# Linear attention's second pass and the output weight splits tied to every fourth step of the attention, and an own buffer for context queries

## The chip, the cores and the metric

The kernel runs on one core of a Trainium2 chip. The core has five engines with a queue of instructions each: TensorE (PE: matmuls, with PEld for its weight loads), VectorE (DVE), ScalarE (ACT), GpSimd (POOL) and SyncE (SP, which here issues most of the DMAs). The metric is the device time of one launch in microseconds. A profiled execution gives a span (first to last instruction) and the durations and waits of single instructions.

## The reference, cut to what matters

A two-layer backbone over 2048 latent tokens behind a prefix of 256 context tokens, width 1024, float32. The change lies in the even layer's mixer, where two head groups run side by side and one output projection reads both:

```
a_x = block_attention(q_x, concat([k_x, k_c]), concat([v_x, v_c]), scale)   # 8 heads, latent tokens see all
a_c = block_attention(q_c, k_c, v_c, scale)                                 # context tokens see context alone
b_x, b_c = gla_bidirectional(latent inputs, context inputs)                 # 4 heads, gated linear attention
y = dot(concat([a * silu(za), rms_norm(b) * silu(zb)]), w_out)
```

`gla_bidirectional` runs a gated recurrence over the chunks forwards and another backwards, the context first in both, and adds the two outputs. `rms_norm` is taken per head of 128.

## The kernel before, in words

The 2304 tokens are 18 tiles of 128. All stages are emitted by one Python program into a scheduler that simulates a timeline: of what is ready in that simulation it takes, for each engine, what was emitted first. The order of each engine's queue, SP's and POOL's too, is fixed by that before the run; on the chip an instruction waits on semaphores at its place, and everything behind it in its queue waits with it. `issue_after(x)` adds one rule: what is emitted inside it, on the engine of x, comes behind x in that engine's queue.

**Attention** (`even_attention`, L867). Four head pairs j, and for each five query blocks nb: the context block (256 queries, 2 key tiles) and four latent blocks (512 queries, 18 key tiles). That is 74 steps a head pair and 296 in all. A step handles one key tile for both heads of the pair: three matmuls a head into a bank "st" (L980 to L982; high and low parts of split operands), the exponential on ACT into one of 14 "apt" tiles (L984, recorded under the helper's line L106), and one addition a head on DVE into the running sums "acc" (L971). The value products "av" (`tail`, L922) follow four steps at a time, when six steps are pending (L992). At the end of a block come "den" (L854) and the division (L859 to L863). Queries load into tile "aq" (L910, L911), which has two slots for all blocks: a load can start when the block before the one before it is done. Key and value tiles load on SP too (L885, L892, L899).

**Linear attention** (`gla`, L686). A first pass goes over the 18 tiles (L714 to L795): gates, decays, the products inside a chunk, and for each tile c a state increment D{c}; rotated queries and the inner output are stored to memory (gQ, gO). Two scans turn the increments into states: forwards on POOL with tile "gsf", backwards on DVE with tile "gsb" (both two slots, L804 to L820). The **second pass** (L821 to L846) then goes over the tiles in backward order, context first. For each: three loads (gQ, gO and the gate half of Un), four matmuls of queries with D{c} (L830), the addition (L831), square (ACT) and reduction (L835), a power of two POOL operations (L200, L202), two products (L838 on DVE, L839 on POOL), four transposes (L842), four scaled copies on ACT into a readout tile that has tag "gsb" as well (L845, recorded under L106), and a store to RT (L846). L830 and L842 use the two banks "gl".

**Output weight splits** (L1028 to L1041). Sixteen pieces of 128x512 of the output weights are loaded into one buffer "wraw" (L380), rounded on ACT, and their rest is taken on DVE (L383). The parts go into tiles that linear attention has left: "gu", "gG", "gqt" and others of its first pass, then D{c} in the order in which the second pass reads them, and the last ones into a new pool "woX".

**Order around the change** (`even_mix`, L1009). The attention is a generator. Its loads and first queries are emitted, then all of linear attention (L1025), then all splits, and then the attention's 20 blocks. What was emitted first goes first where it is ready, so the attention fills what linear attention leaves. From block 18 on (n == 18, L1043) the loop also emits the gate's load and the projection of the two context tiles, which lie in slots of "aq".

Of the kernel before, what the change touches and what calls it, by code (L numbers as in the profile page):

```python
# [10 lines left out]
F32 = mybir.dt.float32  # L11
F32R = mybir.dt.float32r
AF = mybir.ActivationFunctionType
ALU = mybir.AluOpType
# [3 lines left out]
P = 128  # L18
D = 1024
KD = D // P  # L20
# [68 lines left out]
class Kern:  # L89
# [596 lines left out]
    def gla(self, gp, gs, g1, gd, pp, tag):  # L686

        nc = self.nc
# [129 lines left out]

        scan(list(range(NT)), slice(0, 64), nc.gpsimd, "gsf")
        scan(self.back_order(), slice(64, 128), nc.vector, "gsb")  # L820
        for c in self.back_order():  # L821
            qT = self.tl(gs, [P, H, P], "gqT")
            nc.sync.dma_start(qT[:].rearrange("p h t -> p (h t)"), self.gQ[c])
            oi = self.tl(gs, [P, 512], "goi")
            nc.sync.dma_start(oi[:], self.gO[c])
            zb = self.tl(gs, [P, H, P], "gsf")[:].rearrange("p h t -> p (h t)")
            nc.sync.dma_start(zb, self.Un[c, :, 1056:])
            ps = bank()
            for h in range(H):
                nc.tensor.matmul(ps[:, h * P : h * P + P], qT[:, h, :], Dl[c][:, h, :], start=True, stop=True)  # L830
# [7 lines left out]
            nc.vector.tensor_tensor(out=o3, in0=o3, in1=ss[:].unsqueeze(2).to_broadcast([P, H, P]), op=ALU.mult)  # L838
            g.tensor_tensor(out=oi[:], in0=oi[:], in1=zb, op=ALU.mult)  # L839
            ps = bank()  # L840
            for h in range(H):
                nc.tensor.transpose(ps[:, h * P : h * P + P], oi[:, h * P : h * P + P], self.ident[:])  # L842
            ro = self.tl(gs, [P, H, P], "gsb")
            for h in range(H):
                self.act(ro[:, h, :], ps[:, h * P : h * P + P], AF.Copy, scale=gn[:, h : h + 1])  # L845
            nc.sync.dma_start(self.RT[4:8, :, c * P : c * P + P].rearrange("j p t -> p j t"), ro[:])  # L846


    def finish(self, av, dacc, zt, dst, w, ap, pp, tag, lnp=None, bufs=(1, 2), out=None):
# [14 lines left out]
        (out or nc.sync).dma_start(dst, rc[:, :w])  # L864
        return rc

    def even_attention(self, ap, pp):  # L867
# [38 lines left out]

        def queries(j, q0, w):

            q = self.tl(ap, [P, 4, 512], "aq", F32R, bufs=2)
            nc.sync.dma_start(q[:A_QK, :, :w].bitcast(F32), self.QT[2 * j : 2 * j + 2, :, :A_QK, q0 : q0 + w].rearrange("h z p t -> p (h z) t"))  # L910
            return q, nc.sync.dma_start(q[A_QK : A_QK + 1, 0::2, :w].bitcast(F32),  # L911
                                        self.QT[2 * j : 2 * j + 2, 0, A_QK : A_QK + 1, q0 : q0 + w].rearrange("h p t -> p h t"))

        pend, late, O = [], [], {}

# [25 lines left out]
        for j in range(4):  # L941
# [12 lines left out]
            for nb, (q0, w, kts) in enumerate(blocks):  # L954
# [10 lines left out]
                def add(n, pts):  # L965
                    for i in range(2):
                        if n == 0:
                            first[i] = pts[i]
                        else:
                            a = first[i] if n == 1 else acc[i]  # L970
                            nc.vector.tensor_tensor(out=acc[i][:, :w], in0=a[:, :w], in1=pts[i][:, :w], op=ALU.add)  # L971

                for n, kt in enumerate(kts):
                    pts = []
# [2 lines left out]
                    for i in range(2):  # L977
                        qh, ql = Q[:, 2 * i, :], Q[:, 2 * i + 1, :]
                        ps = self.tl(pp, [P, 512], "st", bufs=3)
                        nc.tensor.matmul(ps[:, :w], kh[: A_QK + 1, i, kq], qh[: A_QK + 1, :w], start=True, stop=False)  # L980
# [3 lines left out]
                        self.act(pt[:, :w], ps[:, :w], AF.Exp, scale=A_SCALE)  # L984
                        pts.append(pt)
                    add(n, pts)
                    if n == len(kts) - 1:
# [21 lines left out]
    def even_mix(self, e1, win, hT):  # L1009
# [3 lines left out]
        with ExitStack() as es:  # L1013
            with ExitStack() as esa:
# [5 lines left out]
                with ExitStack() as esg:  # L1020
                    gp = self.pool(esg, "glC", side="right", reuse_waits="tile")
                    gs = self.pool(esg, "glS", bufs=2, side="right", reuse_waits="tile")
                    att = self.even_attention(ap, pp)
                    next(att)
                    self.gla(gp, gs, g1, gd, pp, "gl")  # L1025
                ld = self.pool(es, "woX", bufs=2, side="right", reuse_waits="tile")
                w = {}
                places = [(g1, t) for t in ("gG", "gqt", "gkt", "gkT", "gat", "tri")] + [(gd, f"D{c}") for c in self.back_order()]  # L1028
                for u in range(2 * KD):
                    if u < 2:  # L1030
                        x = self.tl(g1, [P, 1056], "gu", F32R)
                        place = x[:, :512], x[:, 512:1024]
                    elif u < 14:
                        place = [self.tl(q, [P, 512], t, F32R, bufs=1)[:] for q, t in places[2 * u - 4 : 2 * u - 2]]
                    else:
                        place = [self.tl(ld, [P, 512], "wo" + z, F32R)[:] for z in "hl"]
                    n, k = divmod(u, KD)
                    for _ in self.split_steps(w, (k, n), None, self.i["w_out0"][:, k : k + 1, n * 512 : n * 512 + 512], 1, 512, None, 1,
                                              stage=(ap, 1, 512), place=[p.unsqueeze(1) for p in place]):
                        pass  # L1040
# [720 lines left out]
```

## Time and profile before

| | us |
|---|---|
| median of 3 runs | 3669.73 |
| lowest and highest run | 3668.54, 3671.02 |
| the profiled execution's own time | 3676.2 |
| its span | 3674.1 |

The attention stage lies at about 1080 to 1990 us of the span. Linear attention's first pass ends at about 1587, the second pass's last store is issued at 1861.5, and the last "av" group of the attention runs from 1968.7 to 1972.3. Of the page, the busy times show which engine is full; the windows of a stretch show the same for part of the span, with the granted clock of TensorE beside it; a row of the timeline shows an instruction's start, its duration, and in brackets the idle time of its engine just before it with what ended that. "L106" is the helper that issues every ACT operation, so ACT rows go by their tiles.

### The profile page before, as it was taken

The page shows a single profiled execution, that of the slowest core. Times are in us where ns is not written, and L with a number is a line of the kernel's source. Part 1 is how long each engine was busy: PE and PEld are TensorE (multiplying, and loading weights), DVE is VectorE, ACT ScalarE, POOL GpSimd, SP SyncE. Part 2 cuts the span into 40 slices and gives each one's busy share as a digit, 9 for nine tenths or more (in the row PEclk, how much of TensorE's full clock was granted, in tenths as well). Part 3 has the DMA queues.
Part 4 walks back from the last instruction along what each step waited for, and adds up shares of the span by engine and source line. Part 5 has one row for each costly group of instructions (what it writes and reads, how often), then busy time and mean ns, then how long its engine had stood idle before and what let it go on. Part 6 is the DMA issues. An engine that isn't in the chain of part 4 may idle for free.

```text
span 3674.1 us, 51831 instructions
## 1 busy us (share of the span) xinstructions
PE 3565.7 (97%) x18404; PEld 2758.7 (75%) x18404; DVE 2363.0 (64%) x4860; ACT 1437.0 (39%) x2741; POOL 1205.6 (33%) x1336
## 2 busy tenths in 40 slices
PE   8999999999999999999999999999899999999998
PEld 6988998888886666655556878888688887555577
DVE  4677666888876666687664444454578784666721
ACT  5545551111125555555553124444422223555510
POOL 1433330101111212122201233333334443777743
PEclk9999999999999999999999999999999999999899
DMA  7455472222241232243622544455744447788554
GB/s 253 145 155 155 133 210 87 80 73 88 75 137 53 83 98 79 85 115 109 177 67 96 188 161 123 141 157 160 227 146 122 146 120 190 210 215 219 175 178 149
DMA packets 364372, 512.19 MB, mean 139 GB/s; under 512 B 25825, under 2 KB 243889, under 8 KB 358210
## 3 DMA queue, kind: packets, MB, share of 16 engines
q1 hardware_dynamic: 322642, 425.49, 39.8%
q0 software_dynamic: 19872, 55.92, 5.1%
q10 hardware_dynamic: 21600, 27.46, 2.1%
q8 instruction: 146, 2.39, 0.3%
q14 instruction: 112, 0.92, 0.1%
HBM read 329.38 MB, written 179.37 MB: 138 GB/s over the span
## 4 chain that ended last, share of the span: by engine, by line
PE 69%; issue 15%; POOL 5%; DVE 5%; DMA 4%; ACT 2%; SPq 0%; POOLq 0%; DVEq 0%; ACTq 0%
PE av L922 7%; PE gm L129 6%; PE gm L130 6%; PE gm L131 6%; PE st L980 4%; PE st L981 4%; PE st L982 4%; PE st L129 2%; PE st L131 2%; PE st L130 2%; PE pj L131 2%; PE pj L130 2%; PE pj L129 2%; PE o L1456 2%; DMA wraw<-w_od 1%
## 5 line engine op out<-in xcount | busy, mean ns | idle before, releaser
L971 DVE TENSOR_TENSOR acc<-acc,apt 128x512 f32<-128x512 f32 x512 | 364.8, 737 | 153.5 <-ACT apt L106 150.6
L106 ACT ACTIVATE apt<-st 128x512 f32<-128x512 f32 (+1 forms) x592 | 344.6, 594 | 290.5 <-PE st L982 257.4
L662 DVE TENSOR_REDUCE mm<-mx 128x1 f32<-128x512 f32 (+1 forms) x656 | 393.2, 630 | 89.9 <-PE mx L661 81.8
L922 PE MATMUL av<-apt,av 128*64 128x512 f32 (+1 forms) x1184 | 286.4, 599 | 0.0
L980 PE MATMUL st<-aq,akh 97*128 97x512 f32 (+1 forms) x592 | 255.7, 432 | 9.7 <-DMA aq<-QT 6.1
L661 PE MATMUL mx<-mk,mq 96*128 96x512 f32 (+1 forms) x656 | 238.6, 372 | 0.0
L981 PE MATMUL st<-aq,akh 96*128 96x512 f32 (+1 forms) x592 | 236.7, 400 | 0.0
L982 PE MATMUL st<-aq,akl 96*128 96x512 f32 (+1 forms) x592 | 235.3, 398 | 0.0
L1330 DVE CUSTOM_DVE_ANT_1 mx<-mx,mtab 128x217 f32<-128x217 f32 (+11 forms) x576 | 184.6, 338 | 49.2 <-PE mx L1324 37.9
L106 ACT ACTIVATE opt<-opt 128x930 f32<-128x930 f32 (+9 forms) x144 | 119.2, 830 | 248.0 <-POOL opt L1627 141.0
L106 ACT ACTIVATE u<-gm 128x352 f32<-128x352 f32 (+1 forms) x144 | 70.5, 496 | 360.4 <-PE gm L131 208.7
L1587 DVE TENSOR_TENSOR opt<-st,tab 128x64 f32<-128x64 f32 (+10 forms) x576 | 142.8, 316 | 88.2 <-PE st L1424 58.1
L922 PEld LDWEIGHTS av<-apt,av 128*64 128x64 f32 x1184 | 81.9, 138 | 156.4 <-issue 154.8
L980 PEld LDWEIGHTS st<-aq,akh 97*128 97x128 f32 x592 | 113.5, 192 | 101.6 <-issue 49.5
L1462 POOL TENSOR_TENSOR oacc<-oacc,opt 128x682 f32<-128x682 f32 (+10 forms) x144 | 169.8, 1199 | 26.4 <-ACT opt L106 25.1
L982 PEld LDWEIGHTS st<-aq,akl 96*128 96x128 f32 x592 | 114.6, 194 | 25.8
L661 PEld LDWEIGHTS mx<-mk,mq 96*128 96x128 f32 x656 | 122.7, 188 | 11.7
L981 PEld LDWEIGHTS st<-aq,akh 96*128 96x128 f32 x592 | 115.3, 195 | 18.3
L1423 PE MATMUL st<-q,kt 128*128 128x480 f32 (+5 forms) x256 | 99.6, 391 | 23.8 <-DVE opt L1587 18.9
L106 ACT ACTIVATE x<-px,modB,modA 128x128 f32<-128x128 f32 x272 | 99.3, 469 | 58.1 <-PE px L331 46.3
L129 PE MATMUL gm<-w0h,hhi 128*128 128x512 f32 x288 | 116.1, 403 | 0.0
L129 PE MATMUL gm<-w1h,hhi 128*128 128x512 f32 x288 | 115.7, 402 | 0.0
(570 smaller groups left out, 9928.1 us busy)
## 6 DMA issues: line engine op xcount, KB each, us to landing
q<-Q SPq DMA_DIRECT2D x48, 512.0 KB
H<-x ACTq DMA_DIRECT2D x36, 512.0 KB
adaw<-ada_w SPq DMA_DIRECT2D x64, 256.0 KB
x<-H SPq DMA_DIRECT2D x32, 512.0 KB
wraw<-w_od SPq DMA_DIRECT2D x64, 256.0 KB
K1t<-okt POOLq DMA_DIRECT2D x32, 512.0 KB, 7.6
kt<-K1t SPq DMA_DIRECT2D x32, 512.0 KB
mtab<-rpb_q SPq DMA_DIRECT2D x16, 899.0 KB
```

The source lines that it names most:

```text
L106: return self.nc.scalar.activation(out, in_, func, **kw)
L129: self.nc.tensor.matmul(out, lh(k), rh(k), start=j == 0, stop=False)
L130: self.nc.tensor.matmul(out, lh(k), rl(k), start=False, stop=False)
L131: yield self.nc.tensor.matmul(out, ll(k), rh(k), start=False, stop=j == n - 1)
L661: mm = nc.tensor.matmul(ps[:, :w], q[:A_QK, (t % 6) * P : (t % 6) * P + P], k[:A_QK, k0 : k0 + w], start=True, stop=True)
L662: nc.vector.tensor_reduce(out=m[:, t, n : n + 1], in_=ps[:, :w], axis=AX.X, op=ALU.max)
L922: nc.tensor.matmul(O[j, nb][i * 64 : i * 64 + 64, :w], V[j, kt // TT][:, kt % TT, i * 64 : i * 64 + 64], pts[i][:, :w], start=n == 0, stop ...
L971: nc.vector.tensor_tensor(out=acc[i][:, :w], in0=a[:, :w], in1=pts[i][:, :w], op=ALU.add)
L980: nc.tensor.matmul(ps[:, :w], kh[: A_QK + 1, i, kq], qh[: A_QK + 1, :w], start=True, stop=False)
L981: nc.tensor.matmul(ps[:, :w], kh[:A_QK, i, kq], ql[:A_QK, :w], start=False, stop=False)
L982: mm = nc.tensor.matmul(ps[:, :w], kl[:A_QK, i, kq], qh[:A_QK, :w], start=False, stop=True)
L1330: nc.vector.tensor_tensor_reduce(out=s, in0=s, in1=tb[:, ri : ri + rn, ci : ci + cn], scale=1.0, scalar=-3e38, op0=ALU.add, op1=ALU.max, a ...
```

## The change

The second pass becomes a generator in two halves a tile: `enter` (matmuls, addition, square, reduction, power) and `leave` (products, transposes, copies, store), with `fetch` for the loads. One turn of it does `leave` of the tile before, `enter` of this tile, and `fetch` of the next. The weight splits become a generator that splits the piece loaded a turn ago and loads the next. A third generator, `later`, strings both together: six turns of weights, then the second pass with a turn of weights beside every second one, then the rest of the weights.

The attention calls a hook behind every step. From step 166 on, at every fourth, the hook takes one turn of `later`. What it emits on PE, ACT and DVE comes behind the step's last score matmul, its second exponential and its last addition; SP and POOL have no such rule. The first pass and the scans are emitted as before. The context block's queries get a tile "aqc" of their own (256 wide, one slot), and "aq" with its two slots is left to the 512-wide blocks. The gate's load comes behind the last query load on SP.

```diff
@@ gla
-        for c in self.back_order():
+        def fetch(c):
             qT = self.tl(gs, [P, H, P], "gqT")
...
             nc.sync.dma_start(zb, self.Un[c, :, 1056:])
+            return c, qT, oi, zb
+        def enter(c, qT, oi, zb):
             ps = bank()
...
             self.rpow(ss[:], ss[:], 1.0 / 128, EPS)
+            return c, oi, zb, ss
+        def leave(c, oi, zb, ss):
             o3 = oi[:].rearrange("p (h t) -> p h t", h=H)
...
+        def second():
+            order = self.back_order()
+            old, cur = None, fetch(order[0])
+            for c in order[1:] + [None, None]:
+                if old:
+                    leave(*old)
+                old = enter(*cur) if cur else None
+                cur = fetch(c) if c is not None else None
+                yield
+        return second()
@@ even_attention
-            q = self.tl(ap, [P, 4, 512], "aq", F32R, bufs=2)
...
+            q = self.tl(ap, [P, 4, w], "aq" if w == 512 else "aqc", F32R, bufs=2 if w == 512 else 1)
...
+                    hook(mm, ex)
@@ even_mix
+                def hook(mm, ex):
+                    count[0] += 1
+                    if count[0] >= 166 and count[0] % 4 == 2:
+                        with self.tc.issue_after(mm.ins), self.tc.issue_after(ex.ins), self.tc.issue_after(self.add.ins):
+                            next(slow, None)
+                def weights():
...
+                    for u in range(2 * KD + 1):
+                        if raw is not None:
...
+                            self.project_split(raw[:], *place)
+                        if u < 2 * KD:
+                            n, k = divmod(u, KD)
+                            raw = self.tl(ap, [P, 512], "wraw", bufs=1)
+                            nc.sync.dma_start(raw[:], self.i["w_out0"][:, k, n * 512 : n * 512 + 512])
+                        yield
+                def later():
+                    ws = weights()
+                    for _ in range(6):
+                        next(ws)
+                        yield
+                    for n, _ in enumerate(second):
+                        if n % 2 and n < 18:
+                            next(ws)
+                        yield
+                    esg.close()
+                    ld.append(self.pool(es, "woX", bufs=2, side="right", reuse_waits="tile"))
+                    for _ in ws:
+                        yield
+                att = self.even_attention(ap, pp, hook)
+                next(att)
+                second, slow = self.gla(gp, gs, g1, gd, pp, "gl"), later()
                 early = []
                 for n, last in enumerate(att):
                     if n == 18:
-                        gate = self.gate_load(0, 1, self.att_free[:].rearrange("p i w -> p (i w)")[:, :D].bitcast(F32))
+                        for _ in slow:
+                            pass
+                        ld = ld[0]
+                        with self.tc.issue_after(self.qload.ins):
+                            gate = self.gate_load(0, 1, self.att_free[:].rearrange("p i w -> p (i w)")[:, :D].bitcast(F32))
```

More of the change, by code (lines that the diff above doesn't have):

```diff
@@ L865, in finish, with even_attention @@
         return rc
-    def even_attention(self, ap, pp):
+    def even_attention(self, ap, pp, hook):
         nc = self.nc
@@ L970, in add @@
                             a = first[i] if n == 1 else acc[i]
-                            nc.vector.tensor_tensor(out=acc[i][:, :w], in0=a[:, :w], in1=pts[i][:, :w], op=ALU.add)
+                            self.add = nc.vector.tensor_tensor(out=acc[i][:, :w], in0=a[:, :w], in1=pts[i][:, :w], op=ALU.add)
                 for n, kt in enumerate(kts):
@@ L1019, in even_mix @@
                 g1 = self.pool(es, "glA", bufs=2, side="right", reuse_waits="tile")
[L1020 to L1040, printed above, removed]
+                esg = ExitStack()
@@ new lines, in even_mix @@
+                gp = self.pool(esg, "glC", side="right", reuse_waits="tile")
+                gs = self.pool(esg, "glS", bufs=2, side="right", reuse_waits="tile")
+                count, ld, w = [0], [], {}
+                def hook(mm, ex):
[3 more added lines that the diff above has]
+                            next(slow, None)
@@ new lines, in weights @@
+                def weights():
+                    places = [(g1, t) for t in ("gG", "gqt", "gkt", "gkT", "gat", "tri")] + [(gd, f"D{c}") for c in self.back_order()]
+                    raw = None
+                    for u in range(2 * KD + 1):
+                        if raw is not None:
+                            if u < 3:
+                                x = self.tl(g1, [P, 1056], "gu", F32R)
+                                place = x[:, :512], x[:, 512:1024]
+                            elif u < 15:
+                                place = [self.tl(q, [P, 512], t, F32R, bufs=1)[:] for q, t in places[2 * u - 6 : 2 * u - 4]]
+                            else:
+                                place = [self.tl(ld[0], [P, 512], "wo" + z, F32R)[:] for z in "hl"]
+                            n, k = divmod(u - 1, KD)
+                            w[k, n] = [p.unsqueeze(1) for p in place]
+                            self.project_split(raw[:], *place)
[4 more added lines that the diff above has]
+                        yield
```

9 lines of the change are left out of this document (5 added, 4 removed).

## The prediction

> **What bounds the kernel now.** I read the page's head first, then the busy time by stretch of the attention stage (about 1080 to 1990 us of the span), then the waits of TensorE, and then the instructions on both sides of each wait.
>
> ```profile
> span 3674.1 us, 51831 instructions
> PE 3565.7 (97%) x18404; PEld 2758.7 (75%) x18404; DVE 2363.0 (64%) x4860; ACT 1437.0 (39%) x2741; POOL 1205.6 (33%) x1336
> ```
>
> TensorE is the bound of the whole, and a change that moves work without removing any can only win where TensorE stands still or runs at a lower clock. The stage by stretches (columns: us, then busy time and instructions of PE, PEld, DVE, ACT, POOL, then granted clock, DMA share, GB/s):
>
> ```profile
> 1080.00:1587.00 507.00, 503.41 (x2581) 321.10 (x2580) 336.15 (x477) 278.06 (x555) 108.52 (x107) 0.99 0.31 88
> 1587.00:1690.00 103.00, 97.73 (x405) 56.94 (x405) 92.66 (x135) 49.87 (x94) 15.91 (x13) 0.92 0.27 75
> 1690.00:1770.00 80.00, 80.00 (x385) 50.00 (x384) 58.27 (x89) 48.55 (x104) 22.65 (x23) 1.00 0.61 170
> 1770.00:1790.00 20.00, 15.16 (x73) 9.07 (x71) 7.62 (x13) 6.93 (x16) 4.81 (x6) 0.83 0.83 207
> 1790.00:1865.00 75.00, 75.00 (x360) 46.70 (x360) 56.65 (x84) 46.57 (x100) 22.27 (x22) 1.00 0.42 119
> 1865.00:1990.00 125.00, 125.00 (x534) 74.99 (x531) 66.18 (x97) 57.73 (x95) 8.22 (x6) 1.00 0.15 48
> ```
>
> The losses sit in two stretches, 1587 to 1690 and 1770 to 1790; in the others PE is full. The four waits behind them, each the instruction that came after the pause, with the idle time and its releaser in brackets:
>
> ```profile
> 1566.95 0.47 PE L980 MATMUL st<-aq,akh 97*128 97x512 f32 x1 [1.24 <-DMA aq<-QT]
> 1598.22 0.50 PE L980 MATMUL st<-aq,akh 97*128 97x512 f32 x1 [1.55 <-ACT apt L106]
> 1674.80 2.07 PE L830 MATMUL gl<-D,gqT 128*128 128x128 f32 x8 [3.71 <-ACT gsb L106]
> 1782.14 0.77 PE L980 MATMUL st<-aq,akh 97*128 97x512 f32 x1 [4.84 <-DMA aq<-QT]
> ```
>
> I call them A, B, C and D. Together 1.24 + 1.55 + 3.71 + 4.84 = **11.3 us** idle. After B, C and D the clock falls as well (same columns as above; the clock is the third number from the end):
>
> ```profile
> 1590.00:1600.00 10.00, 8.45 (x36) 4.36 (x33) 9.69 (x16) 5.03 (x11) 2.23 (x3) 0.95 0.32 100
> 1600.00:1610.00 10.00, 10.00 (x38) 5.14 (x37) 9.78 (x15) 3.48 (x7) 2.65 (x2) 0.70 0.29 79
> 1650.00:1660.00 10.00, 10.00 (x44) 6.02 (x44) 9.65 (x15) 5.31 (x10) 0.00 (x0) 1.00 0.00 0
> 1670.00:1680.00 10.00, 6.29 (x21) 5.07 (x20) 7.83 (x13) 5.75 (x15) 0.00 (x0) 0.71 0.27 79
> 1680.00:1690.00 10.00, 10.00 (x41) 4.95 (x40) 4.34 (x8) 3.37 (x9) 2.92 (x3) 0.78 0.12 28
> 1780.00:1790.00 10.00, 7.86 (x29) 4.90 (x29) 1.98 (x3) 2.39 (x4) 1.02 (x2) 0.66 0.76 192
> ```
>
> Missing clock times length: B (0.05 + 0.30) x 10 = 3.5, C (0.29 + 0.22) x 10 = 5.1, D 0.34 x 10 = 3.4, **12.0 us** in all, which I count as time lost (an upper end). So 23.3 us of the stage are lost at four places. That is the most that the change can win if it adds nothing.
>
> **The change part by part.**
>
> *The context buffer (A and D).* Each head pair starts with a 256-wide context block of two steps, whose queries held one of the two "aq" slots. So the first 512-wide block's queries could load only when the block before the context block was done.
>
> ```profile
> 1771.16 10.89 DMA aq<-QT
> 1724.09 0.45 SPq L910 DMA_DIRECT2D aq<-QT  x1
> ```
>
> The first row is the chain's: the load took 10.89 us, beside two short steps. The second is the load issued one slot earlier, for the context block of the last head pair: it went out some 45 us ahead of its use. With a buffer of its own for context, the slot sequence moves by one: the 512-wide queries go out at that earlier place, and their 10.89 us lie beside a whole block of 18 steps. Block and load stay the same size, so nothing is added but SBUF. The rows show nothing that would be late next. Gain: 1.24 + 4.84 + 3.4 = **9.5 us**. On SP the context loads now queue no later than before.
>
> *The weight splits (B).* One step loads a piece (SP), rounds it on ACT and subtracts on DVE, 16 times. Now load and split of a piece are one call, four steps, apart.
>
> ```profile
> 1597.05 0.63 ACT L106 ACTIVATE gkt<-wraw 128x512 fp32r<-128x512 f32 x1 [2.63 <-DMA wraw<-w_out]
> 1673.60 1.14 ACT L106 ACTIVATE gsb<-gl,gn 128x128 f32<-128x128 f32 x4 [3.98 <-DVE gsb L815]
> ```
>
> The first row is B: ACT waited 2.63 us for a piece with the step's exponentials queued behind, and TensorE then waited for those. Four steps of distance are about 9.5 us (below), which is more than 2.63. So this wait goes: **5.0 us** (1.55 + 3.5). The 16 rounds and 16 subtractions stay and move.
>
> *The second pass (C).* The second row is C: the copies of the first readout tiles use the slots of tile "gsb", which the backward scan on DVE (L814 to L816) also uses. They were put in ACT's order at the place where the scan was expected to be done, and the scan came 3.98 us late. Now the pass begins later. Where, comes from the count of L982, two per step (column x):
>
> ```profile
> 1080.00:1587.00 507.00, 123.79 (x314) 0.99 0.31 88
> 1612.00:1662.00 50.00, 16.59 (x42) 1.00 0.22 63
> 1690.00:1770.00 80.00, 23.65 (x60) 1.00 0.61 170
> ```
>
> At 1587, when the first pass ends, 314 / 2 = 157 steps are done. A step without second-pass work takes 50 / 21 = 2.38 us. The first call is at step 166 (about 1608), six calls go to the weights, so the first matmuls of the pass come at step 190 (1587 + 33 x 2.38 = 1666) and the first copies at step 194 (1675). Without stalls ahead of them, and with more steps done by 1587 because A is gone, both move up by a few us. The scan ended at about 1674 with its work, in the 89 us before, shared like this:
>
> ```profile
> L971 DVE TENSOR_TENSOR acc<-acc,apt 128x512 f32<-128x512 f32 x57 | 39.7, 719 | 1.0
> L815 DVE TENSOR_TENSOR gsb<-gsb,D 64x512 f32<-64x512 f32 x16 | 13.4, 836 | 0.5
> L816 DVE TENSOR_TENSOR D<-gsb,fac 64x512 f32<-64x512 f32 x16 | 12.0, 750 | 0.5
> ```
>
> It loses two chunks of second-pass work in front of it (six operations of about 0.7 us, 4.2 us) and keeps about five splits, so it ends near 1670. The margin at step 194 is a few us either way. I take it that C goes (3.71 + 5.1 = **8.8 us**), and keep its staying as a rival.
>
> *What the moved work costs where it now lies.* The operations of a chunk and a split, whose count doesn't change:
>
> ```profile
> L830 PE MATMUL gl<-D,gqT 128*128 128x128 f32 x144 | 20.0, 284 | 3.7 <-ACT gsb L106 3.7
> L842 PE MATMUL gl<-ident,goi 128*128 128x128 f32 x72 | 10.8, 272 | 0.0
> L838 DVE TENSOR_TENSOR goi<-goi,gss 128x512 f32<-128x512 f32 x18 | 12.8, 714 | 0.0
> L839 POOL TENSOR_TENSOR goi<-goi,gsf 128x512 f32<-128x512 f32 x18 | 23.8, 1322 | 32.9 <-DVE goi L838 31.0 <-ACT apt L106 2.0
> L106 ACT ACTIVATE gsb<-gl,gn 128x128 f32<-128x128 f32 x72 | 20.5, 376 | 4.4 <-DVE gsb L815 4.0 <-PE gl L842 0.4
> L106 ACT ACTIVATE D<-wraw 128x512 fp32r<-128x512 f32 x9 | 5.9, 661 | 0.0
> L383 DVE TENSOR_TENSOR D<-wraw,D 128x512 fp32r<-128x512 f32 x9 | 6.1, 681 | 0.0
> ```
>
> Between 1690 and 1770 the kernel already runs one chunk every four steps: 30 steps and 56 / 8 = 7 chunks in 80 us, PE full, clock 1.00. The steps alone are 30 x 2.38 = 71.4, so a chunk costs (80 - 71.4) / 7 = 1.2 us of TensorE. That is the very rhythm that the change writes down, and TensorE pays the 1.2 us there or here: **0**. DVE's part of four steps is 8 additions of 0.72, three second-pass operations and half a split, about 8.2 of 10.7 us; ACT has 8 exponentials, a square, four copies and half a split, also below 10.7. The chunk's three loads and one store on SP, and its two small power operations on POOL, move with it; only PE, ACT and DVE are held behind the step, SP and POOL are free to go earlier. On SP a load that waits for a slot may now stand ahead of others, but queries have some 45 us of lead.
>
> New waits at the 27 calls are shown by no row. From below: none, as in those 80 us (less than none is excluded, since TensorE's work is the same). From above: at each of the 18 second halves TensorE stands while L838 and L839 run, 0.71 + 1.32 = 2.0 us, 36 us in all. The nearest row says 0.0 before L842 in 18 of 18 chunks, so I stay near the lower end and keep one stall of B's size, **5.0 us**.
>
> Tail: the pass ends with call 25 at step 262 of 296 and the last split with call 27 at step 270, before the projection starts at step 278, so the end of the stage isn't later. If that cover were gone, the loads of the context tiles would stand at the end, about as long as A's load.
>
> **Sum**: 9.5 + 5.0 + 8.8 - 5.0 = 18.3 us. The profiled execution took 3676.2 us; 3676.2 - 18.3 = 3657.9. It stands 6.5 us above the median 3669.7, so the forecast in the runs' own measure is **3651 us** (-0.5%).
>
> The stretch 1587 to 1690 can be checked by rate: 34.5 steps (x69 in a view of L982) are 82 us, about four chunks 5 us, so 16 us of 103 are lost, against 13.9 by B and C. The 2 us between are the room below.
>
> [...] B's clock row shows 0.70 after a pause of only 1.55 us. [...]
>
> **The rivals.**
>
> 1. *The scan still decides (C stays).* For it: the margin at step 194 is a few us and the copies stand in ACT's order ahead of exponentials. Against: each bank of "gl" now has four steps to come free. 8.8 us less: 3660 us. Chance 0.22.
> 2. *B's low clock doesn't hang on B's pause.* 3.5 us stay: 3655 us. For it: 1.55 us is the shortest pause that is followed by one, and A's 1.24 isn't. Against: it begins right behind the pause. Chance 0.05. [...]
> 3. *DVE takes over (no visible change).* The scan's some 36 us (13.4 + 12.0, and L814 with some 11 like them) now meet steps at full pace from 1587 on; DVE was busy 9.65 of 10 us between 1650 and 1660. If the exponentials wait for additions, what B and C gave comes back as slower steps: 13.8 us, with A and D's gain cut by the 5.0 kept, about 3665 us. Against: in that same row TensorE was full at 1.00 with 44 matmuls. Chance 0.10.
> 4. *Slower: the second halves block TensorE.* The transposes L842 stand in TensorE's order close behind the step, and wait for L838 on DVE and L839 on POOL, which run behind that step's addition. 18 x 2.0 = 36 us instead of the 5.0: 3651 + 31 = 3682 us, more where the clock falls. It decides from (18.3 + 5.0 + 7) / 18 = 1.7 us a chunk on. For it: nothing ties the transposes to POOL's pace but an order fixed ahead of the run, and C shows such an order being 4 us off. Against: 0.0 before L842. Chance 0.13.
>
> That the change doesn't move what it says could be: loads and POOL work aren't held by it. But then they run earlier, which changes no term of the sum.
>
> **How the numbers follow.** Forecast 3651 us, chance 0.50; rivals 0.22, 0.05, 0.10, 0.13. A measurement here tells apart about 0.2%, 7.3 us, so "faster" is below 3662.4. Faster: 0.50 + 0.05, most of the first rival (0.17) and a little of the third (0.02), 0.74; same 0.13; slower 0.13. The range reaches from the whole 23.3 and the 2 us above (3676.2 - 25.3 - 6.5 = 3644, rounded out to 3643) to the third rival with its spread (3668); outside it lie the slower rival and a few in a hundred below.
>
> **What would show it.** Right: no idle before L980 that ends with "DMA aq<-QT"; query loads of the 512-wide blocks issued a block ahead; no ACT wait for "wraw"; L830 first at about 1660 to 1675; granted clock 1.00 from 1590 on; four steps with a chunk at 10.7 us. Wrong: ACT idle before "gsb" with a releaser on L815 (rival 1), steps above 2.5 us with DVE full from 1590 to 1670 (rival 3), idle before L842 (rival 4). The sum is wrong as a whole if stages behind 1990 us change, which it takes as fixed.

## The result, and the profile after

The changed kernel takes 3651.67 us (median; 3650.16 to 3652.14) beside 3668.54 us of the kernel before: a ratio of 0.9949, interval 0.9938 to 0.996. The forecast was 3651. Of the profiled execution, the span and the busy times:

```profile
span 3649.9 us, 51809 instructions
PE 3552.6 (97%) x18404; PEld 2750.0 (75%) x18404; DVE 2355.6 (65%) x4860; ACT 1433.1 (39%) x2741; POOL 1200.8 (33%) x1336
```

The same number of matmuls takes less time. The stage by the same stretches as in the prediction (us, then busy time of PE, PEld, DVE, ACT, POOL, granted clock, DMA share, GB/s):

```profile
1080.00:1587.00 507.00, 504.59 (x2589) 321.03 (x2588) 334.74 (x478) 277.31 (x563) 101.95 (x106) 1.00 0.30 87
1587.00:1690.00 103.00, 98.83 (x437) 58.09 (x437) 97.71 (x143) 52.48 (x92) 11.42 (x9) 0.97 0.26 75
1690.00:1770.00 80.00, 80.00 (x400) 50.76 (x398) 53.19 (x84) 48.07 (x105) 23.69 (x25) 1.00 0.67 183
1770.00:1790.00 20.00, 20.00 (x94) 11.34 (x91) 16.89 (x25) 11.78 (x25) 8.37 (x8) 1.00 0.45 140
```

1770 to 1790 is full now (15.16 us of 20 before), and in 1587 to 1690 there are 437 matmuls in place of 405. One loss is left in that stretch, and TensorE's waits from 1095 to 1990 name it (total us, times, longest; no other in this view is over 0.4 us):

```profile
PE st L1003 <- ACT apt L106: 4.2, 1, 4.2
```

Lines behind the change are numbered higher: L980 of before is L1003 here, L830 is L835, L831 is L836, L838 and L839 are L847 and L848, L842 is L851, L910 is L932, L971 is L994. The four waits A, B, C and D of the prediction are gone. The one of 4.2 us is new; I call it E. The timeline around it (start, duration, in brackets the idle time before with its releaser):

```profile
1666.65 0.69 DVE L815 TENSOR_TENSOR gsb<-gsb,D 64x512 f32<-64x512 f32 x1
1667.37 0.69 DVE L816 TENSOR_TENSOR D<-gsb,fac 64x512 f32<-64x512 f32 x1
1668.09 0.69 DVE L814 TENSOR_TENSOR gsb<-gsb,fac 64x512 f32<-64x512 f32 x1
1668.81 0.69 DVE L836 TENSOR_TENSOR goi<-gl,goi 128x512 f32<-128x512 f32 x1
...
1669.54 0.63 ACT L106 ACTIVATE ge<-goi 128x512 f32<-128x512 f32 x1 [5.48 <-DVE goi L836]
...
1670.71 0.79 PE L1003 MATMUL st<-aq,akh 97*128 97x512 f32 x1 [4.17 <-ACT apt L106]
```

Read it upwards. TensorE waits for an exponential. ACT stood 5.48 us at the square of the second pass's first tile ("ge"), with the exponentials behind it in its queue. The square waits for the addition L836, and that stands on DVE behind operations of the backward scan (L814 to L816). DVE itself has no gap. In the 10 us stretches around E:

```profile
1650.00:1660.00 10.00, 10.00 (x46) 5.75 (x44) 9.65 (x16) 5.42 (x9) 0.00 (x0) 1.00 0.35 99
1660.00:1670.00 10.00, 6.53 (x32) 3.57 (x28) 9.62 (x15) 1.06 (x2) 0.00 (x0) 1.00 0.10 35
1670.00:1680.00 10.00, 9.29 (x28) 5.03 (x28) 9.72 (x16) 5.54 (x11) 1.93 (x2) 0.66 0.00 1
```

DVE (third time) is full and ACT almost idle; behind the pause the clock falls to 0.66. E costs 4.17 us idle and 0.34 x 10 = 3.4 us of clock, 7.6 us.

**A sharper measure than the whole time.** The medians of one kernel differ by some us from set to set (start 182 below: 3644.36 and 3650.29). Much of that lies outside the attention: what is left of the span without the stretch defined here runs from 2787.3 to 2800.2 us over the fourteen profiles. So I also use the *stretch* from the first to the last value product of the attention ("first and last start" in the row of its line), here of the kernel before and of the changed one:

```profile
L922 PE MATMUL av<-apt,av x1184: 379/592/1116, 1096.6 to 1971.7; 128*64 128x512 f32 x192, 128*64 128x256 f32 x6
```

```profile
L945 PE MATMUL av<-apt,av x1184: 379/592/1116, 1093.8 to 1951.0; 128*64 128x512 f32 x192, 128*64 128x256 f32 x6
```

1971.7 - 1096.6 = 875.1 us before, 1951.0 - 1093.8 = 857.2 after: **17.9 us less**, of 16.9 in the medians. A second profiled execution of the changed kernel gave 856.9, and start 182 gave 851.7 and 851.5, so by these two repeats the stretch tells about 0.5 us apart. Idle time and missing clock from 1095 to 1990, counted as in the prediction, fell from 23.5 to 8.3 us; that is 15.2 of the 17.9. (The two profiled spans differ by 24.2 us; the 6.3 beside the 17.9 lie outside the stretch, within the scatter just given.)

### The profile page after: what moved, and what is told of

Read it like the earlier page. It is cut to its first block, busy times and chain, and to the rows that moved or that the text cites. A ratio compares the mean times of both kernels' runs of the same rounds, so it can differ in the third digit from the quotient of the medians.

```text
span 3649.9 us, 51809 instructions
## 1 busy us (share of the span) xinstructions
PE 3552.6 (97%) x18404; PEld 2750.0 (75%) x18404; DVE 2355.6 (65%) x4860; ACT 1433.1 (39%) x2741; POOL 1200.8 (33%) x1336
## 4 chain that ended last, share of the span: by engine, by line
PE 71%; issue 15%; DVE 5%; POOL 4%; DMA 4%; ACT 2%; POOLq 0%; SPq 0%; DVEq 0%; ACTq 0%
PE av L945 7%; PE gm L129 6%; PE gm L131 6%; PE gm L130 6%; PE st L1003 4%; PE st L1004 4%; PE st L1005 4%; PE o L1515 2%; PE st L129 2%; PE st L131 2%; PE st L130 2%; PE st L1482 2%; PE pj L129 2%; PE pj L131 2%; PE pj L130 2%
## 5 line engine op out<-in xcount | busy, mean ns | idle before, releaser
L994 DVE TENSOR_TENSOR acc<-acc,apt 128x512 f32<-128x512 f32 x512 | 368.7, 743 | 163.1 <-ACT apt L106 160.4
L945 PE MATMUL av<-apt,av 128*64 128x512 f32 (+1 forms) x1184 | 279.1, 594 | 0.0
L1003 PE MATMUL st<-aq,akh 97*128 97x512 f32 x576 | 249.2, 433 | 4.2 <-ACT apt L106 4.2
L1004 PE MATMUL st<-aq,akh 96*128 96x512 f32 x576 | 230.0, 399 | 0.0
L1005 PE MATMUL st<-aq,akl 96*128 96x512 f32 x576 | 229.6, 399 | 0.0
L1521 POOL TENSOR_TENSOR oacc<-oacc,opt 128x682 f32<-128x682 f32 (+9 forms) x144 | 169.8, 1202 | 28.9 <-ACT opt L106 27.7
L1003 PEld LDWEIGHTS st<-aq,akh 97*128 97x128 f32 x576 | 109.3, 190 | 86.9 <-issue 45.0
L1004 PEld LDWEIGHTS st<-aq,akh 96*128 96x128 f32 x576 | 110.7, 192 | 17.5
L1482 PE MATMUL st<-q,kt 128*128 128x480 f32 (+5 forms) x256 | 99.7, 391 | 22.5 <-DVE opt L1646 17.9
L815 POOL TENSOR_TENSOR gsf<-gsf,D 64x512 f32<-64x512 f32 x17 | 24.8, 1459 | 276.8 <-DVE D L792 276.8
```

Of the source, the lines that this page charges most:

```text
L945: nc.tensor.matmul(O[j, nb][i * 64 : i * 64 + 64, :w], V[j, kt // TT][:, kt % TT, i * 64 : i * 64 + 64], pts[i][:, :w], start=n == 0, stop ...
L994: self.add = nc.vector.tensor_tensor(out=acc[i][:, :w], in0=a[:, :w], in1=pts[i][:, :w], op=ALU.add)
```

## The experiments

Twelve experiments, two of them repeats, in three sets, each set timed beside the kernel before (3668.55, 3667.61 and 3670.05 us). "Lost" is idle time plus missing clock of TensorE between 1095 and 1990, to about 0.5 us.

| kernel | median us | ratio to before, interval | stretch us | lost us |
|---|---|---|---|---|
| before | 3668.5 | | 875.1 | 23.5 |
| changed | 3651.67 | 0.9949, 0.9938 to 0.996 | 857.2 | 8.3 |
| changed, again | 3654.34 | 0.9961, 0.9949 to 0.9974 | 856.9 | 7.4 |
| buffer alone | 3653.32 | 0.996, 0.9948 to 0.9972 | 860.1 | 9.7 |
| hook alone (start 166) | 3652.79 | 0.9959, 0.9945 to 0.9973 | 859.6 | 7.1 |
| hook alone, start 182 | 3656.47 | 0.9968, 0.9956 to 0.998 | 858.5 | 6.2 |
| start 158 | 3658.61 | 0.9968, 0.9958 to 0.9979 | 859.6 | 9.7 |
| start 174 | 3653.45 | 0.9951, 0.9935 to 0.9966 | 855.0 | 6.4 |
| start 182 | 3644.36 | 0.9938, 0.9925 to 0.995 | 851.7 | 1.9 |
| start 182, again | 3650.29 | 0.9948, 0.9935 to 0.996 | 851.5 | 2.0 |
| start 206, every second step | 3645.16 | 0.9938, 0.9923 to 0.9953 | 850.7 | 1.3 |
| pass ahead, splits in turns | 3655.71 | 0.997, 0.9958 to 0.9982 | 860.4 | 9.7 |
| first splits ahead, pass from 206 | 3648.58 | 0.9943, 0.993 to 0.9957 | 857.1 | 8.4 |
| backward scan on POOL | 3658.0 | 0.9972, 0.9962 to 0.9982 | 867.3 | 19 |

**The theory at this point:** the four waits went as predicted, and E is what the prediction kept as "one stall", with a cause: the hook comes while the scan still fills DVE. Rival: E is a plain part of the hook's cost, wherever it starts, and the parts are worth what their terms say. First the parts alone.

*Buffer alone.* The kernel before, with the buffer's edit (the two loads behind it then take the whole tile in place of `:w`):

```diff
-            q = self.tl(ap, [P, 4, 512], "aq", F32R, bufs=2)
+            q = self.tl(ap, [P, 4, w], "aq" if w == 512 else "aqc", F32R, bufs=2 if w == 512 else 1)
...
```

> The kernel before with the context buffer alone; linear attention's second pass and the weight splits stay ahead of the attention. Theory (the stalls A and D are the query load's, and the buffer removes them): no idle before the score matmuls that ends with the query load, and 9.5 us less than before (1.24 + 4.84 idle, 3.4 clock), about 3659 us; B and C stay. Rival (the load was hidden anyway, TensorE filling the gap with linear attention, and the stall only moves): within 2 us of before, about 3668 us.

It gave 15.0 us of stretch, more than its term of 9.5. A and D are gone, and on top of that C is halved. ACT's rows (kernel with the buffer alone):

```profile
1607.88 0.63 ACT L106 ACTIVATE ge<-goi 128x512 f32<-128x512 f32 x1 [4.79 <-DVE goi L831]
...
1617.47 0.63 ACT L106 ACTIVATE gat<-wraw 128x512 fp32r<-128x512 f32 x1 [3.87 <-DMA wraw<-w_out]
...
1682.12 1.14 ACT L106 ACTIVATE gsb<-gl,gn 128x128 f32<-128x128 f32 x4 [4.82 <-DVE gsb L815]
```

ACT still waits for the scan in the last row, and 4.82 us at that, but TensorE loses 0.76 + 1.97 us idle and 1.7 of clock there, where C was 8.8. And B's place shows two causes now: weight pieces (the cause the prediction gave) and, 10 us ahead of the row shown, the addition L831 of a tile of the second pass. TensorE stands still for 1.50 us directly behind the first row, and for 1.41 us at 1625.55, behind a further split (2.15 us for its piece) and a further square. The second cause is in the profile of before as well, 4 us ahead of B's row, and the prediction didn't read it:

```profile
1592.87 0.63 ACT L106 ACTIVATE ge<-goi 128x512 f32<-128x512 f32 x1 [2.02 <-DVE goi L831]
```

*Hook alone.* The changed kernel without the buffer:

```diff
-            q = self.tl(ap, [P, 4, w], "aq" if w == 512 else "aqc", F32R, bufs=2 if w == 512 else 1)
+            q = self.tl(ap, [P, 4, 512], "aq", F32R, bufs=2)
...
```

> The changed kernel with the context queries back in the shared two slots. Theory: the load's stalls come back at the heads' borders, 9.5 us more than the changed kernel, about 3661 us, with an idle time of 4 to 5 us before a score matmul that ends with the query load. Rival (the gain is the hook's alone): 3652 us, like the changed kernel.

It gave 15.5 us, again more than its terms: expected were 9.5 us over the changed kernel, and its stretch is 2.4 us over it. B and C are gone, A (0.87 us) and D are still there but smaller (kernel with the hook alone, its chain and its timeline):

```profile
1752.31 8.03 DMA aq<-QT
```

```profile
1760.42 0.47 PE L1003 MATMUL st<-aq,akh 97*128 97x512 f32 x1 [1.98 <-DMA aq<-QT]
```

The load took 8.03 us in place of 10.89, 2.86 less, and that is the whole difference of the pause (4.84 - 1.98 = 2.86). E is nearly absent. The two parts are not additive: 15.0 + 15.5 = 30.5 against 17.9 together.

*Another start.* The prediction's choice of step for the second pass, moved (the turns that are left at block 18 are then emitted there at once):

```diff
-                    if count[0] >= 166 and count[0] % 4 == 2:
+                    if count[0] >= 182 and count[0] % 4 == 2:
```

> The changed kernel with the first turn at step 182 instead of 166; what is left at step 278 is emitted there at once. Theory (the changed kernel's one stall, 4.2 us and 3.4 us of clock near 1670, is the first square on ACT waiting for an addition on DVE that stands behind the backward scan): the scan is over when the second pass begins at step 206, the stall goes, 7.6 us less, about 3644 us. Rival (the stall hangs on the block border at which it lies, or on the rhythm): it stays or moves along, 3652 us.

E vanished and the stretch fell by 5.5 us, of 7.6 expected. The 10 us windows of E's time in the kernel that starts at 182:

```profile
1660.00:1670.00 10.00, 10.00 (x44) 5.45 (x42) 9.65 (x15) 6.39 (x11) 0.00 (x0) 1.00 0.12 39
1670.00:1680.00 10.00, 10.00 (x46) 5.76 (x44) 9.87 (x17) 5.41 (x9) 1.33 (x1) 1.00 0.10 29
```

DVE is as full as in the changed kernel (9.65 and 9.87 us of 10), and TensorE doesn't lose a tenth. So a full DVE alone cost nothing here; it cost where something that ACT needed at once stood in DVE's queue (4.17 us idle at E).

*The scan taken off DVE.* The other way to remove E, with the start left at 166:

```diff
-        scan(self.back_order(), slice(64, 128), nc.vector, "gsb")
+        scan(self.back_order(), slice(64, 128), nc.gpsimd, "gsb")
```

> The changed kernel with the backward scan on POOL instead of DVE, everything else the same. Theory: DVE is no longer full from 1600 to 1690 (the scan was some 36 us of it), the addition before the first square isn't late, the stall goes, about 3644 us. Rival (POOL's slower scan, 51 operations of about 1.3 us, is itself late for the second pass): a wait on POOL takes the stall's place, 3652 us or more.

This came out the opposite way: 867.3 us of stretch, 10 more than the changed kernel. From 1590 to 1690 (groups; busy us, mean ns), first the kernel with the scan on POOL, then the changed one:

```profile
L994 DVE TENSOR_TENSOR acc<-acc,apt 128x512 f32<-128x512 f32 x62 | 75.4, 1268 | 5.0 <-ACT apt L106 5.0
...
L815 POOL TENSOR_TENSOR gsb<-gsb,D 64x512 f32<-64x512 f32 x16 | 25.7, 1606 | 1.3
```

```profile
L994 DVE TENSOR_TENSOR acc<-acc,apt 128x512 f32<-128x512 f32 x67 | 47.0, 736 | 3.3 <-ACT apt L106 2.4
```

The additions on DVE took 1268 ns each in place of 736 while POOL worked beside them. So DVE stayed as full as before (94.5 us of 100 from 1590 to 1690, and 94.7 in the changed kernel), and E stayed too, for 4.39 us of TensorE. ACT, in the kernel with the scan on POOL:

```profile
1650.59 0.63 ACT L106 ACTIVATE gkt<-wraw 128x512 fp32r<-128x512 f32 x1 [6.64 <-DMA wraw<-w_out]
...
1682.43 0.63 ACT L106 ACTIVATE ge<-goi 128x512 f32<-128x512 f32 x1 [5.70 <-DVE goi L836]
```

The second row is E's instruction, with no scan on DVE: what it needs is behind other work in DVE's queue, here the slowed additions. The first row is one of two new waits for weight pieces (6.64 and 6.51 us; TensorE lost 2.56 and 2.42 us behind them): the piece's load starts at 1647.89, when DVE is done with the piece before it. Neither ACT nor TensorE waits for the scan on POOL, so the rival's cause isn't it either, though its time was met. The run therefore doesn't part the scan from any other backlog on DVE; it shows another thing about the two engines (last section).

*The changed kernel again*, unchanged, for the scatter:

> The changed kernel once more, beside the next three on the same chip. All theories: 3652 us, the stall near 1670 with about 4 us idle and 3 us of clock in its trace.

Its stretch is 856.9. E is there again, 4.2 us idle and 1.7 of clock, and a wait of 1.0 us for POOL's L848 before a transpose is the only one of that kind in the two executions of the changed kernel.

*How E depends on the start.* With 158 and 174 in the same line:

> The changed kernel with the first turn at step 158, so that the second pass begins at step 182. Theory (the stall near 1670 is the first square of the second pass behind DVE's scan): it begins some 20 us before the scan ends, so stalls of the kind come at more than one turn; idle and clock lost between 1590 and 1720 above the 7 to 8 us of the start at 166, about 3655 us. Rival (the place of the start doesn't matter): 3652 us and the same loss.

> The changed kernel with the first turn at step 174, second pass from step 198. Theory: the first turn of the pass comes at about 1680, when the scan has just ended, so the loss lies between that of 166 (7 to 8 us) and that of 182 (2 us), about 3647 us. Rival: as at 166, 3652 us.

> The start at 182 once more. Theory: again no idle above 1 us and no lost clock between 1095 and 1960; about 3645 us. Rival (the first run was lucky): a stall near 1670 to 1700, 3652 us.

The second pass's first matmuls L835 and the scan's last L815 ("first and last start") for starts 158 and 182:

```profile
L815 DVE TENSOR_TENSOR gsb<-gsb,D x17: 689/690/1656, 1181.7 to 1685.9; 64x512 f32<-64x512 f32 x17
...
L835 PE MATMUL gl<-D,gqT x144: 273/275/377, 1645.9 to 1853.7; 128*128 128x128 f32 x144
```

```profile
L815 DVE TENSOR_TENSOR gsb<-gsb,D x17: 687/689/690, 1178.8 to 1670.3; 64x512 f32<-64x512 f32 x17
...
L835 PE MATMUL gl<-D,gqT x144: 274/275/378, 1701.1 to 1889.9; 128*128 128x128 f32 x144
```

| start | first L835 | scan's last L815 | E: idle + clock, us | stretch us |
|---|---|---|---|---|
| 158 | 1645.9 | 1685.9 | 4.91 + 3.4 | 859.6 |
| 166 | 1661.6 | 1676.3 | 4.17 + 3.4 | 857.2 |
| 174 | 1681.8 | 1673.7 | 2.27 + 3.45 | 855.0 |
| 182 | 1701.1 | 1670.3 | 0 | 851.6 |

The more of the second pass lies in the scan's time, the later the scan ends and the longer E. (Executions begin some us apart; counted from each one's first value product, the scan's last L815 comes 589.0, 582.5, 579.6 and 576.3 us later.) With 158 the copies wait for the scan again as well, 3.65 us on ACT, so there is more than one stall, as expected. The medians alone don't show this order: 3651.67 and 3654.34 for 166, 3653.45 for 174. In all three kernels of this table that have E, it is the same instruction that waits; here with start 174, ACT and then TensorE:

```profile
1686.87 0.63 ACT L106 ACTIVATE ge<-goi 128x512 f32<-128x512 f32 x1 [2.57 <-DVE goi L836]
...
1688.03 0.80 PE L1003 MATMUL st<-aq,akh 97*128 97x512 f32 x1 [2.27 <-ACT apt L106]
```

So E isn't a fixed price of the hook: the rival falls, the theory holds for the kernels with the scan on DVE. Why 166 was too early with the buffer and not without it, is told by the first pass (forward scan on POOL, whose last addition needs the first pass's last increment; before, then changed):

```profile
L815 POOL TENSOR_TENSOR gsf<-gsf,D x17: 1272/1287/1717, 1174.7 to 1586.5; 64x512 f32<-64x512 f32 x17
```

```profile
L815 POOL TENSOR_TENSOR gsf<-gsf,D x17: 1268/1577/1725, 1173.9 to 1599.3; 64x512 f32<-64x512 f32 x17
```

With the buffer, the first pass ends some 13 us later. It is the buffer that does it: this last L815 starts at 1599.2 with the buffer alone and at 1583.9 with the hook alone. At 1587 the attention is 4.5 steps further with the buffer (x323 of L1004, shown further below, in place of the x314 of L982 before), some 10.7 us of steps. That is more than A's pause of 1.24 us could give, so the order in which the scheduler mixes the two has moved as well; how, no run here isolates. The scan follows the first pass, the hook follows the attention's steps: the same edit pushes them together. With the hook alone the scan's last L815 is at 1663.5, the first L835 at 1666.4.

*The buffer's worth once E is gone.* Hook alone with start 182:

> The hook alone (context queries in the shared slots), with the first turn at step 182. It shows what the buffer is worth where the scan's stall is absent with and without it. Theory now: the buffer and the place of the second pass aren't independent; at step 166 the buffer's gain of some 4.5 us (as the idle and clock of the load's stalls came to with the hook alone) was paid back by the scan's stall, so here it is 4.5 us over the kernel that starts at 182, about 3649 us. Rival (the prediction's step: the buffer is worth 9.5 us): about 3654 us.

```profile
PE st L1003 <- DMA aq<-QT: 3.1, 2, 2.2
PE st L1003 <- ACT apt L106: 1.5, 1, 1.5
```

858.5 us against 851.6 with the buffer: the buffer is worth 6.9 us, more than I had expected here and less than its term of 9.5. With start 166 it is worth 859.6 - 857.0 = 2.6, since it brings E with it.

*Which of the hook's two halves takes B away?* The second pass emitted at once as in the kernel before, the splits in turns from step 182; and the other way round, the first six turns of weights (five splits) at once and the pass at its place of start 182 (step 206):

```diff
-                    if count[0] >= 166 and count[0] % 4 == 2:
+                    if count[0] >= 182 and count[0] % 4 == 2:
...
                 second, slow = self.gla(gp, gs, g1, gd, pp, "gl"), later()
+                for _ in second:
+                    pass
+                second = iter(range(19))
```

> Buffer, and splits in turns from step 182 on, but the second pass emitted whole ahead of the attention as in the kernel before. Theory (C is the second pass being placed before DVE's scan is done): waits of ACT or TensorE on tiles of the scan near 1680 come back, about 4 to 9 us over the kernel that starts at 182, 3649 to 3653 us. Rival (only the splits' loads matter): 3644 us.

```diff
-                    if count[0] >= 166 and count[0] % 4 == 2:
+                    if count[0] >= 206 and count[0] % 4 == 2:
...
                 second, slow = self.gla(gp, gs, g1, gd, pp, "gl"), later()
+                for _ in range(6):
+                    next(slow)
```

> The kernel that starts the second pass at step 206, but its first six turns of weights (six loads, five splits) emitted at once ahead of the attention, as in the kernel before. Theory (B is ACT waiting for a weight piece with exponentials behind it): ACT waits of 2 us and more on the weight load come back at about 1600, 2 to 5 us over the kernel that starts at 182, 3646 to 3649 us. Rival (the splits were never the trouble, the second pass beside them was): 3644 us and no such wait that TensorE sees.

Each half by itself leaves a stall at B's place. With the pass ahead, ACT waits for additions of the pass: 6.12 us for the first tile's, which costs TensorE 0.79 us, and 1.70 us for the second tile's, with TensorE's pause of 1.76 us behind it:

```profile
1607.55 0.63 ACT L106 ACTIVATE ge<-goi 128x512 f32<-128x512 f32 x1 [6.12 <-DVE goi L836]
...
1623.79 0.63 ACT L106 ACTIVATE ge<-goi 128x512 f32<-128x512 f32 x1 [1.70 <-DVE goi L836]
```

```profile
1625.47 0.50 PE L1003 MATMUL st<-aq,akh 97*128 97x512 f32 x1 [1.76 <-ACT apt L106]
```

C's place is back too, as expected: the copies wait 2.48 us for the scan's L815, the square behind them 3.52 us for its addition, and TensorE loses 3.22 us idle and 1.7 of clock near 1687. That is about half of the 9.7 us lost.

With the splits ahead it waits for a weight piece, and TensorE 3.25 us for ACT:

```profile
1611.89 0.63 ACT L106 ACTIVATE gkt<-wraw 128x512 fp32r<-128x512 f32 x1 [3.55 <-DMA wraw<-w_out]
...
1613.06 0.80 PE L1003 MATMUL st<-aq,akh 97*128 97x512 f32 x1 [3.25 <-ACT apt L106]
```

Four kernels with the buffer, by stretch (the first, buffer alone, has all sixteen splits ahead; the one below it the first five):

| | splits ahead | splits in turns |
|---|---|---|
| pass ahead | 860.1 | 860.4 |
| pass in turns, first at step 206 | 857.1 | 851.6 |

The splits in turns give nothing as long as the pass is ahead, and 5.5 us when it isn't; that is more than I had expected for them.

*The rhythm.* Double pace, begun at step 206:

```diff
-                    if count[0] >= 166 and count[0] % 4 == 2:
+                    if count[0] >= 206 and count[0] % 2 == 0:
```

> The changed kernel with the first turn at step 206 and a turn at every second step, so the second pass runs from step 218 to 254. Theory (TensorE pays about 1.2 us a tile wherever it lies; only what stands in front of a late producer costs): no new idle, 3645 us; DVE has some 5.3 us of work in the 6.0 us of two steps. Rival (the rhythm of four is needed, closer second halves block TensorE on POOL and DVE): idle before the transposes or the score matmuls between 1730 and 1850, 3650 us and more.

850.7 us of stretch and 1.3 us lost. A turn at every second step costs nothing that the stretch shows, where the pass begins behind the scan; the double pace from an early start wasn't run. Start 182 and this kernel have the best stretches of all, 5.5 and 6.4 us under the changed kernel's mean of 857.05. In the whole time their ratios (0.9938, 0.9948; 0.9938) stand beside 0.9949 and 0.9961, and the intervals overlap.

## Why the prediction was right

**The bound and the sum.** TensorE's lost time was the gain: 15.2 us of it went, and the stretch is 17.9 shorter, where the sum said 18.3. The 2.7 us between are of the size of the 2 us that the check by rate had left unexplained; the runs don't settle what they are. That the total agrees so well is partly luck: the buffer and the hook alone gave 5.5 and 6.7 us more than their terms (9.5 and 5.0 + 8.8 - 5.0), and together 12.6 less than their sum.

**The buffer (9.5).** Right in mechanism: no wait for "aq" is left, and the 512-wide queries go out a block ahead. SP's rows in the changed kernel, two latent blocks' loads and a context block's:

```profile
1487.90 0.32 SPq L932 DMA_DIRECT2D aq<-QT  x1
...
1548.11 0.45 SPq L932 DMA_DIRECT2D aq<-QT  x1
...
1550.80 0.30 SPq L932 DMA_DIRECT2D aqc<-QT  x1
```

The third row goes out when a context block is done. The latent block behind it begins then, at about 1551, and its load is the first row, some 60 us ahead. The size depends on what else is there: 15.0 alone, 6.9 beside a hook that starts at 182, 2.6 beside one at 166. The step that failed is "the rows show nothing that would be late next". What was late next was the scan, by some 13 us at the first pass's end.

**The splits (5.0).** The wait of before went, and with the pass in turns the splits are worth 5.5. But "the wait for the piece" was one of two causes at the same place (the row at 1592.87 above is the other); had only the splits been moved, nothing would have been won (860.4 beside 860.1). ACT did still wait for a piece twice in the changed kernel, 1.11 and 1.30 us, against the sign that the prediction gave; TensorE didn't notice.

**The second pass (8.8) and the stall that was kept (5.0).** C's own instruction, the copies into "gsb", waited for the scan no more: they stand four steps behind the matmuls, and by then the scan was done. But the same scan now stopped the first square, through DVE's queue instead of through the slots. That is rivals 1 and 3 crossed, and it cost 7.6 us (5.9 in the second execution) in place of the 5.0 kept without a name. The size was near; that the stall came at the first square and not at the transposes, for which it was kept, makes this term luck. The working that missed it is the position: the prediction set the scan's end near 1670 and the first matmuls at 1666 and checked the margin at the copies, at step 194. It should have checked it at the first instruction that passes through DVE, at step 190. The count of L1004 (two a step) shows how far the attention had got at 1587:

```profile
1080.00:1587.00 507.00, 127.56 (x323) 1.00 0.30 87
```

323 / 2 = 161.5 steps in place of 157, so the hook came early (1661.6) while the scan came late (last L815 at 1676.3).

**The moved work (0).** Right. From 1690 to 1865 TensorE is full at clock 1.00; from 1690 to 1770, 30 steps (x60 of L1004) and 8 tiles (x64 of L835) pass, beside 30 steps and 7 tiles before. Nothing waits before the transposes:

```profile
L851 PE MATMUL gl<-ident,goi x72: 270/272/329, 1684.6 to 1867.4; 128*128 128x128 f32 x72
```

**The rivals.** The first held in its cause (the scan) and not in its place. The second is false: no clock is missing where B was. Before, 1600 to 1610 stood at 0.70; in the changed kernel:

```profile
1590.00:1600.00 10.00, 10.00 (x63) 7.32 (x60) 7.70 (x14) 4.30 (x8) 0.68 (x1) 1.00 0.35 111
1600.00:1610.00 10.00, 10.00 (x45) 5.79 (x45) 9.71 (x12) 5.30 (x10) 2.42 (x2) 1.00 0.45 123
```

So the lost clock went with the pause of 1.55 us. The third, as slower steps, is false: DVE was full, but TensorE stayed at 10.00 of 10 us with 44 and 46 matmuls at start 182. The fourth is false: no transpose waited in one execution, one waited 1.0 us in the other, and at twice the pace none waited.

## What to carry to other kernels

Work that is tied to a step count should be placed well behind the producer that it depends on (starts 182 and 206), or perhaps be tied to that producer itself, which no run here tries: an edit that speeds up the counted loop moves the hook ahead, and may slow the producer (here the loop was 4.5 steps further at 1587, and the first pass ended some 13 us later). When two edits cure waits in the same in-order queue, measure each alone and both together; here one half alone was worth nothing (860.4 beside 860.1), and two that were worth about 15 us each made 18. Check the margin at the first moved instruction that goes through the busy engine: here the exponentials behind its consumer waited with it (5.48 us on ACT, 4.17 on TensorE).

## What the runs showed of the hardware

**DVE's additions beside POOL.** With the backward scan on POOL, the 128x512 additions on DVE took 1268 ns on average in place of 736, beside POOL operations on 64x512 of 1358 to 1606 ns (means of L814, L816 and L815). When the scan was over (at 1679.5) they took 0.68 us again, and a product that reads one input from PSUM (L883, at 1630.85) took 0.68 us beside a running POOL operation. The rows give the size; the cause they don't show.

**Short pauses and the clock.** A clock of 0.50 followed pauses of TensorE of 1.41 us (buffer alone), 1.55 (before), 1.76 (pass ahead), 1.98 (hook alone) and 2.27 (start 174), and did not follow others of 1.40 (start 182 again), 1.50 (buffer alone), 1.54 and 2.22 (hook alone with start 182). Lost clock came in pieces of about 1.7 us: 1.7, 3.4 or 5.1; with the pass ahead, one of 1.7 is 0.50 from about 1626.6 to 1630.0, so 3.4 us long. So in these traces a pause of 1.40 to 2.27 us was followed by a loss of 1.7 to 3.5 us more or by none, and its length alone didn't tell which.

**One load, two durations.** The same query load took 10.89 us before and 8.03 with the hook alone; the pause behind it shrank by just that. In both stretches the DMA engines were about 0.95 busy, at 230 GB/s for 11 us (1771 to 1782) and 220 GB/s for 8 us (1752 to 1760), so 2.5 and 1.8 MB moved, of which the load itself is 0.8. Less other traffic beside it fits the shorter time; no run changes that traffic alone.
